# Two layers of experts: products in ordered phases of one array tiling, gathers and scatters of the last layer done another way

## The chip, the cores and the metric

One core of a Trainium2 chip runs the whole program in one launch. The metric is the device time of one execution in microseconds, the median of several runs. TensorE (PE) multiplies; a product's stationary operand is loaded by PEld beside it. DVE is VectorE, ACT ScalarE, POOL GpSimd, SP SyncE, and SPq and POOLq are the queues of DMA issues of the last two. All transfers share 16 DMA engines.

## The reference

The program is two transformer blocks on 512 tokens ("latents") of 1024 channels, with 256 tokens of context beside the first block. The first block has two layers, each a mixer (two attentions, a convolution, gates, an output product) and then a feed-forward of 16 experts, where each expert chooses its tokens; the context has the experts in layer 0 alone. The second block has two more attentions and an output product. All is float32. The change lies in the experts:

```python
def expert_choice_ffn(h, w_router, w_g, w_u, w_d):
    B, n, D = h.shape
    cap = CAPACITY_FACTOR * n // N_EXPERTS         # 64 latents, 32 of the context
    logits = jnp.einsum('bnd,de->ben', h, w_router, preferred_element_type=jnp.float32)
    aff = jax.nn.softmax(logits, axis=1)
    gate, idx = lax.top_k(aff, cap)
    bi = jnp.arange(B)[:, None, None]
    xs = h[bi, idx]
    a = jnp.einsum('becd,edf->becf', xs, w_g)      # w_g, w_u, w_d: 16 x 1024 x 1024
    u = jnp.einsum('becd,edf->becf', xs, w_u)
    y = jnp.einsum('becf,efd->becd', jax.nn.silu(a) * u, w_d)
    return jnp.zeros_like(h).at[bi, idx].add(y * gate[..., None].astype(y.dtype))
```

Here `h` is a norm of the rows with a scale and a shift per channel, and the result, times a gate per channel, is added to the rows.

## The kernel before

The kernel is written with tile pools. A scheduler in the language's compiler gives each engine its order: it takes instructions by the priority of the program's order and by when it reckons them ready, so that work of later lines can stand between work of earlier ones. Semaphores are made from the data's dependences.

**Order of the program** (`run`, from L48): mixer of layer 0 on the latents, then on the context, `experts` for both streams, mixer of layer 1 on the latents, `experts_local`, then block 2.

**Weights of the experts** (`ring_start`, `ring_open`, `ring_load`, from L834). An expert has three matrices of 4 MB: gate, up, down. They stream through a ring of slots of 2 MB, half a matrix each, ten slots in layer 0 and nine in layer 1. A load is two DMAs of 1 MB on SP's queue (L865), and waits until the products that read the slot's last content are done. The first slots are filled during the mixer that goes before.

**One expert** (`up` L1211, `act` L1222, `down_ps` L1237). The tokens' channel-major norms `xT` are stationary, the weights stream. A latent expert has 64 tokens, so two halves of the columns stand side by side in the array (tiling 128*64, `h` = 2, 512 columns each); a context expert has 32, so four quarters do (128*32, 256 columns each). Gate and up products go to PSUM, `act` makes 2 * silu(a) * u with ACT and DVE, turns it with transposes on TensorE (128*128) and copies it to SBUF, and the down product takes it as stationary.

**Layer 0** (`experts` L1269). Per expert: gate product of the latents, of the context, up product of both, `act` of both, down product of both. `gather` (L1192) fetches 128 rows (two latent experts or four of the context) by an indirect DMA on POOL's queue, transposes them in 8 pieces and applies scale and shift (`affine`). `down` (L1249) scales the output by gate and channel gate and adds it to the rows in DRAM with an indirect accumulating DMA. The latents' expert 0 goes ahead of the stage, in `expert0` (L1260).

**Layer 1** (`experts_local` L1297). The rows and their norms stay in SBUF (`kept`, filled in `project` L1016 to L1068). `gather(g)` makes a one-hot matrix of two experts' tokens and multiplies it with the four tiles of norms; `scatter(e, y)` splits the 64 x 1024 output into a high and a low part and multiplies each by a one-hot matrix, 16 products with 64 rows, whose sums DVE adds to the rows (L1350). Both halves of the output's columns lie in different halves of the partitions.

**Choice** (`choose` L1111): ranks the tokens on DVE and gives each expert's indices and gates (`ig`), and for streams that fetch by DMA the indices as integers (`gi`, `si`).

Of the kernel before, what the change touches and what calls it, by code (L numbers as in the profile page):

```python
# [8 lines left out]
FP32 = mybir.dt.float32  # L9
# [20 lines left out]
class Stream:  # L30
    """One of the two token streams: latents or context."""
# [6 lines left out]
class Kernel:  # L38
    def __init__(self, tc, A, out):
        self.tc, self.nc, self.A, self.out = tc, tc.nc, A, out  # L40
        self.uid = 0
        self.flip = 0
        self.pend = None
        self.pcols = 768
        self.late = None
        self.wada = {}

# [58 lines left out]
    def blend(*parts):  # L106
        """The steps of several (generator, steps), spread evenly over each other."""
# [22 lines left out]
    def copy(self, out, in_):  # L130
        """A plain copy, on the scalar engine and the vector engine in turn."""
# [6 lines left out]
    def transpose(self, out, in_):  # L138
        p = in_.shape[0]
        self.nc.tensor.transpose(out, in_, self.ident[:p, :p])  # L140
# [24 lines left out]
    def exp(self, pool, out, x, w):  # L165
        """exp(x) for x <= 0 on the vector engine, to float32's accuracy: 2^k * e^r, |r| <= ln(2) / 2."""
# [14 lines left out]
    def split(self, src, hi, lo):  # L181
        """src = hi + lo, both in the 12 significant bits of float32r."""
# [3 lines left out]
    def wblock(self, pool, src):  # L186
        """A block of weights [K, 256]: per 512 rows its two float32r parts [128, 4, 256]."""
# [10 lines left out]
    def mm3(self, ps, lhs, rhs, lsel, rsel):  # L198
        """ps = sum over k tiles of lhs^T rhs, each a list of two parts by k tile."""
# [70 lines left out]
    def adaln(self, l, r, pool):  # L270
        """Columns r * 2048 to (r + 1) * 2048 of both streams' modulation of layer l, in 17 steps."""
# [35 lines left out]
    def ada_load(self, l, r, pool, *tiles):  # L307
        """Loads pieces [128, 1024] of w_ada, unless they are there."""
# [18 lines left out]
    def norm(self, xt, junk, xn=None):  # L327
        """Token-major rows scaled by their rsqrt of the mean square, in place or into xn; the last tile's on its own."""
# [9 lines left out]
    def scale(self, out, in_, col, i):  # L338
        """Rows by a column, on the vector engine and the scalar engine in turn."""
# [17 lines left out]
    def hT(self, pool, h, xn, G, S):  # L357
        """The modulated norm of a stream, channel-major, in two parts; KT steps."""
# [21 lines left out]
    def hT_raw(self, raw, xn):  # L380
        """The norm without its modulation, channel-major."""
# [29 lines left out]
    def heads_block(self, pool, ps, dst, ss, t, nh, tabs, g):  # L411
        """dst = rope(ps * g) for nh heads of one token tile; ss = their sums of squares."""
# [58 lines left out]
    def k_parts(self, tp, kh, kl, j):  # L471
        """Head j of the transposed keys tp [128, n] into the doubled parts kh, kl [128, n]."""
# [6 lines left out]
    def k_block(self, pool, kr, ss, nt, nh, kh, kl):  # L479
        """Normalises the roped keys kr [128, nt, nh * 64] and writes their parts."""  # L480
# [11 lines left out]
    def kv_block(self, pool, w, h, st, tabs, g, kh, kl, V, kr=None):  # L492
        """Two key heads and two value heads of a stream from a block [ka | va] of w_in."""
# [1117 lines left out]
```

## Time and profile before

| | us |
|---|---|
| time, median of 3 runs | 3030.7 (3026.78 to 3032.99) |
| span of the profiled execution, first to last instruction | 3023.8 |
| TensorE busy | 2895.2 (96%) |
| DVE busy | 1415.6 (47%) |
| ACT busy | 957.7 (32%) |
| POOL busy | 110.1 (4%) |
| mean granted TensorE clock, as a share of full speed | 0.977 |
| bytes moved | 629.24 MB, mean 208 GB/s |

The profiled execution has no time of its own beside its span. Times in the trace are microseconds from the span's start. Matmuls are pipelined, so the busy time of one is longer than its distance to the next; where work stands in blocks, the distance between the blocks' starts is what it costs. A share of the DMA engines near 1 means that packets were in flight on all 16 throughout; it can pass 1 a little, since packets overlap.

### The profile page before, as it was taken

How to read it: one execution, taken by the hardware profiler on the slowest of the kernel's cores; microseconds unless marked ns; L12 is line 12 of the kernel's file. 1: busy time of each engine (PE TensorE's matmuls, PEld its weight loads, DVE VectorE, ACT ScalarE, POOL GpSimd, SP SyncE). 2: the span in 40 equal slices, each digit the busy share in tenths (PEclk: the TensorE clock that was granted, in tenths of full speed). 3: DMA queues.
4: the chain of work that ended last, by engine and by line, in shares of the span. 5: the costliest groups of instructions: out<-in, count | busy, mean ns of one | idle time of the engine just before them, and what ended most of it. 6: DMA issues, size and time to landing. Idle time of an engine off the chain costs nothing.

```text
span 3023.8 us, 45171 instructions
## 1 busy us (share of the span) xinstructions
PE 2895.2 (96%) x18117; PEld 1866.4 (62%) x18117; DVE 1415.6 (47%) x3807; ACT 957.7 (32%) x1950; POOL 110.1 (4%) x135
## 2 busy tenths in 40 slices
PE   7999999999998999999979999999799999889999
PEld 3777777678895443433347777778744433338878
DVE  4655565348764111111146555654523232237885
ACT  4444454224552000000044444543200000015663
POOL 0100000011001011100000000000000000000000
PEclk8999999999998999999999999999899999999999
DMA  8321111668457999999573211114689999953221
GB/s 296 123 69 56 56 42 50 206 210 308 136 174 255 389 403 397 402 395 368 180 262 116 68 56 56 43 53 141 260 348 397 414 361 363 370 196 107 57 84 57
DMA packets 272646, 629.24 MB, mean 208 GB/s; under 512 B 24324, under 2 KB 148948, under 8 KB 272436
## 3 DMA queue, kind: packets, MB, share of 16 engines
q1 hardware_dynamic: 259396, 595.31, 53.5%
q0 software_dynamic: 12016, 27.86, 3.2%
q8 instruction: 143, 2.34, 0.3%
q10 hardware_dynamic: 1024, 3.18, 0.3%
q14 instruction: 67, 0.55, 0.1%
HBM read 606.30 MB, written 19.99 MB: 207 GB/s over the span
## 4 chain that ended last, share of the span: by engine, by line
PE 73%; issue 14%; DMA 6%; DVE 4%; ACT 1%; SPq 0%; POOL 0%; POOLq 0%; ACTq 0%; DVEq 0%
PE mm L204 13%; PE mm L205 12%; PE mm L206 12%; PE au L1217 8%; PE tp L140 5%; PE yp L1243 4%; PE S L521 4%; PE mm L611 4%; DMA x<-ylat,silat 4%; PE S L520 3%; PE S L282 3%; PE tx L1330 2%; PE yp L1348 1%; DVE xt L1350 1%; PE S L1038 1%
## 5 line engine op out<-in xcount | busy, mean ns | idle before, releaser
L204 PE MATMUL mm<-hhi,whi 128*128 128x512 f32 (+1 forms) x928 | 341.6, 368 | 0.0
L184 DVE TENSOR_TENSOR wlo<-wraw,whi 128x1024 fp32r<-128x1024 f32 x234 | 285.7, 1222 | 107.0 <-ACT whi L183 102.4
L206 PE MATMUL mm<-hhi,wlo 128*128 128x512 f32 (+1 forms) x928 | 335.1, 361 | 0.0
L205 PE MATMUL mm<-hlo,whi 128*128 128x512 f32 (+1 forms) x928 | 333.6, 360 | 0.0
L183 ACT ACTIVATE whi<-wraw 128x1024 fp32r<-128x1024 f32 x234 | 247.1, 1059 | 185.5 <-PE mm L205 106.7
L1243 PE MATMUL yp<-we,hT 128*32 128x256 f32 (+1 forms) x2016 | 294.2, 496 | 10.3 <-ACT hT L134 4.9
L1217 PE MATMUL au<-we,xT 128*64 128x512 f32 x1024 | 236.5, 597 | 0.0
L204 PE MATMUL mm<-whi,hhi 128*128 128x256 f32 x736 | 218.8, 298 | 10.6 <-ACT qr L423 6.6
L1217 PE MATMUL au<-we,xTlat 128*64 128x512 f32 x960 | 227.1, 599 | 0.3
L205 PE MATMUL mm<-wlo,hhi 128*128 128x256 f32 x736 | 212.8, 290 | 2.1 <-DVE wlo L184 2.1
L206 PE MATMUL mm<-whi,hlo 128*128 128x256 f32 x736 | 212.5, 290 | 0.0
L1243 PEld LDWEIGHTS yp<-we,hT 128*32 128x32 f32 (+1 forms) x2016 | 99.1, 124 | 182.4 <-issue 144.5
L563 ACT ACTIVATE PT<-tp 128x384 f32<-128x384 f32 (+2 forms) x392 | 142.6, 407 | 211.6 <-PE tp L140 209.7
L204 PEld LDWEIGHTS mm<-hhi,whi 128*128 128x128 f32 x928 | 176.3, 190 | 32.1 <-issue 4.4
L206 PEld LDWEIGHTS mm<-hhi,wlo 128*128 128x128 f32 x928 | 176.0, 190 | 25.9 <-issue 1.1
L205 PEld LDWEIGHTS mm<-hlo,whi 128*128 128x128 f32 x928 | 176.3, 190 | 24.9 <-issue 1.5
L535 ACT ACTIVATE P<-S,mx,sc 128x768 f32<-128x768 f32 (+5 forms) x192 | 151.9, 792 | 70.9 <-DVE mx L532 67.6
L204 PEld LDWEIGHTS mm<-whi,hhi 128*128 128x128 f32 x736 | 143.0, 194 | 26.9 <-ACT qr L423 8.5
L1217 PEld LDWEIGHTS au<-we,xT 128*64 128x64 f32 x1024 | 70.6, 137 | 129.2 <-issue 126.1
L205 PEld LDWEIGHTS mm<-wlo,hhi 128*128 128x128 f32 x736 | 143.0, 195 | 5.4 <-DVE wlo L184 2.7
L206 PEld LDWEIGHTS mm<-whi,hlo 128*128 128x128 f32 x736 | 142.7, 194 | 4.0 <-issue 2.8
L1226 ACT ACTIVATE th<-au 128x512 f32<-128x512 f32 (+1 forms) x47 | 24.6, 524 | 378.3 <-PE au L1217 378.3
(326 smaller groups left out, 4830.5 us busy)
## 6 DMA issues: line engine op xcount, KB each, us to landing
we<-in_w_e_gate_dram SPq DMA_DIRECT2D x128, 1024.0 KB, 11.5
we<-in_w_e_up_dram SPq DMA_DIRECT2D x128, 1024.0 KB, 11.1
we<-in_w_e_down_dram SPq DMA_DIRECT2D x128, 1024.0 KB, 11.0
wraw<-in_w_in_dram SPq DMA_DIRECT2D x166, 512.0 KB, 3.7
wada<-in_w_ada_dram SPq DMA_DIRECT2D x96, 512.0 KB, 6.1
wraw<-in_w_branch_dram SPq DMA_DIRECT2D x36, 512.0 KB, 3.4
wraw<-in_w_out_dram SPq DMA_DIRECT2D x32, 512.0 KB, 3.9
xt<-in_x_dram SPq DMA_DIRECT2D x8, 512.0 KB, 9.2
```

Source lines behind the costliest of these rows:

```text
L140: self.nc.tensor.transpose(out, in_, self.ident[:p, :p])
L183: self.nc.scalar.activation(hi, src, ACTF.Copy)
L184: self.nc.vector.tensor_sub(lo, src, hi.bitcast(FP32))
L204: nc.tensor.matmul(ps, lh, rh, start=k == 0, stop=False)
L205: nc.tensor.matmul(ps, lh, rl, start=False, stop=False)
L206: nc.tensor.matmul(ps, ll, rh, start=False, stop=k == n)
L521: nc.tensor.matmul(S[:, at:at + w], lhs[row], kl[row, k0:k0 + w], start=False, stop=True)
L535: nc.scalar.activation(P, S[:, c0:c1], ACTF.Exp, bias=mx[:, 1:2], scale=sc, accum_out=mx[:, 2:3])
L563: self.nc.scalar.activation(PT[:, s0:s0 + j - i, qc:qc + 128], tp[:, i * 128:j * 128].rearrange("p (s c) -> p s c", c=128), ACTF.Copy)
L611: nc.tensor.matmul(O[64 * j:64 * j + 64, a:b], v, PTs[j][:, slot, a:b], start=i == 0, stop=i == last, skip_group_check=True)
L1217: self.nc.tensor.matmul(ps[j * st.cap:(j + 1) * st.cap], st.xT[:, kt, s0:s0 + st.cap], w[kt // 4][:, kt % 4, j * st.w:(j + 1) * st.w], sta ...
L1243: self.nc.tensor.matmul(ps[o * st.cap:(o + 1) * st.cap], hT[:, j * 128 + q * st.cap:j * 128 + (q + 1) * st.cap], w[kt // 4][:, kt % 4, o * ...
```

## The change

Three things. First, an order of TensorE's work in both expert stages: `pe_phase` opens a phase, and `pe_run` adds for given instructions an edge to each instruction of the phase before, without a semaphore, so that the scheduler keeps the phases apart. In layer 0 a round is: down product of the latents' last expert and gate and up products of the next (128*64); gate and up of the context and its last down product (128*32); all transposes (128*128). Fetches are issued one group ahead of the transposes that use them. In layer 1 a round is the last expert's down product and the next one's gate and up (128*64), then scatter, gather and transposes (128*128).

Second, the norms of layer 1 go to DRAM as in layer 0 (two buffers instead of four tiles kept), and `gather` is the one of layer 0. `choose` makes the integer indices for this stream too.

Third, the scatter takes two experts at once: high and low part of each half of the columns are stacked to 128 rows (`parts`), and the sums of both experts are formed in PSUM before DVE adds them, half of them after each of the next two experts. In block 2 the norm's result has tiles of its own.

The comments and docstrings that the diff takes out are left out here.

```diff
+    def pe_phase(self):
+        self.pe_before, self.pe_now = self.pe_now, []
+    def pe_run(self, insts):
+        insts = [i.ins for i in insts]
+        for i in insts:
+            for b in self.pe_before:
+                self.tc.add_manual_dep(
+                    i, b.name, mybir.DependencyInfo(mybir.DependencyClass.NoSync, mybir.DependencyReason.DATA),
+                    reason="phase")
+        self.pe_now += insts
...
 project:
-            xo = xp.tile([128, D], FP32, name="xn", bufs=nx)
+            xo = p.tile([128, D], FP32, name="xn", bufs=2)
             self.scale(xo, xt[t], r, t)
-            if dst:
-                nc.gpsimd.dma_start(self.dr[f"xn{st.name}{l}"][t * 128:t * 128 + 128], xo)
-            else:
-                self.kept.append((xt[t], xo))
+            nc.gpsimd.dma_start(self.dr[f"xn{st.name}{l}"][t * 128:t * 128 + 128], xo)
+            if not dst:
+                self.kept.append(xt[t])
...
 choose:
+        st.gi = cp.tile([128, NE // h], U32, name="gi" + sfx)
         if st.xs is not None:
+            for j in range(h):
+                nc.vector.tensor_copy(st.gi[j * cap:(j + 1) * cap],
+                                      ig[:cap, 0].rearrange("p (g j) -> p j g", j=h)[:, j])
             nc.vector.tensor_copy(ig[64:128], ig[:64])
...
-    def gather(self, st, g, p, p_x, bufs=1):
-        xg = p.tile([128, D], FP32, name="xg" + st.name, bufs=1)
-        nc.gpsimd.indirect_dma_start(
-            out=xg, out_offset=None, in_=self.dr[f"xn{st.name}{st.l}"],
+    def fetch(self, st, g, p):
+        st.xg = p.tile([128, D], FP32, name="xg" + st.name, bufs=1)
+        self.nc.gpsimd.indirect_dma_start(
+            out=st.xg, out_offset=None, in_=self.dr[f"xn{st.name}{st.l}"],
             in_offset=bass.IndirectOffsetOnAxis(ap=st.gi[:, g:g + 1], axis=0))
+    def gather(self, st, p, p_x, bufs=1):
...
 up, down_ps (the products of the first and the last k tile):
+            if kt in (0, KT - 1):
+                self.pe_run(r)
...
 act is cut in two, act (up to t) and act_turn:
+        self.pe_run([self.transpose(tp[:, j * 128:(j + 1) * 128], t[:, j * 128:(j + 1) * 128]) for j in range(nj)])
...
 experts:
+            for st in sts:
+                self.expert_setup(l, st, xs[st.name], p)
+                self.fetch(st, 0, p)
+            hT, wd = {}, None
+            def turned(st, e):
+                if e % st.h == 0 and e < NE:
+                    st.xT = self.gather(st, p, p_x, 2 if st is lat else 1)
+                    if e + st.h < NE:
+                        self.fetch(st, e // st.h + 1, p)
+            for st in sts:
+                turned(st, 0)
+            for e in range(NE + 1):
+                self.pe_phase()
+                if lat in hT:
+                    self.down(lat, wd, hT[lat], e - 1, p, p_y)
+                t = {}
+                if e < NE:
+                    w = [self.ring_get(i, e) for i in range(2)]
+                    for st in sts:
+                        if st is cx:
+                            self.pe_phase()
+                        if e or st is cx:
+                            t[st] = self.act(st, *[self.up(st, w[i], e, p_a) for i in range(2)], p)
+                if cx in hT:
+                    self.down(cx, wd, hT[cx], e - 1, p, p_y)
+                self.pe_phase()
+                if e < NE:
+                    hT = {}
+                    if lat in t:
+                        hT[lat] = self.act_turn(lat, t[lat], p, p_x)
+                    turned(lat, e + 1)
+                    hT[cx] = self.act_turn(cx, t[cx], p, p_x)
+                    turned(cx, e + 1)
+                    wd = self.ring_get(2, e)
...
 experts_local:
+            def parts(e, ps):
+                y = p.tile([128, 512], FP32, name="y")
                 nc.vector.scalar_tensor_tensor(y, in0=ps, scalar=st.ig[:, 1, e:e + 1], in1=st.gt2,
                                                op0=ALU.mult, op1=ALU.mult)
+                one = p.tile([128, NL], F32R, name="two", bufs=3)
+                nc.vector.tensor_scalar(one, row, st.ig[:, 0, e:e + 1], None, op0=ALU.is_equal)
+                yp = p.tile([128, 2, 512], F32R, name="yp", bufs=3)
+                for o in range(2):
+                    a, b = slice(64 * o, 64 * o + 64), slice(64 - 64 * o, 128 - 64 * o)
+                    nc.scalar.activation(yp[a, o], y[a], ACTF.Copy)
+                    nc.vector.tensor_sub(yp[b, o], y[a], yp[a, o].bitcast(FP32))
+                return one, yp
+            def scatter(ys, tiles):
+                for t in tiles:
+                    for o in range(2):
+                        ps = p_y()
+                        self.pe_run([nc.tensor.matmul(ps, one[:, t * 128:(t + 1) * 128], yp[:, o],
+                                                      start=i == 0, stop=i == len(ys) - 1)
+                                     for i, (one, yp) in enumerate(ys)])
+                        x = self.kept[t][:, 512 * o:512 * o + 512]
+                        nc.vector.tensor_add(x, x, ps)
+                        yield
...
+            for e in range(NE):
+                self.pe_phase()
+                if hT is not None:
+                    ys.append(parts(e - 1, self.down_ps(st, wd, hT, p_y())))
+                t = self.act(st, *[self.up(st, self.ring_get(i, e), e, p_a) for i in range(2)], p)
+                self.pe_phase()
+                if e % 2 == 0 and len(ys) == 2:
+                    work, ys = scatter(ys, range(4)), []
+                for _ in range(4):
+                    next(work, None)
+                if e % 2 and e + 1 < NE:
+                    turned(e // 2 + 1)
+                hT = self.act_turn(st, t, p, p_x)
+                wd = self.ring_get(2, e)
+            self.pe_phase()
+            ys.append(parts(NE - 1, self.down_ps(st, wd, hT, p_y())))
+            self.drive(scatter(ys, range(4)))
```

## Rows read from the trace of the kernel before

**Rows 1.** TensorE's timeline, layer 0: start us, us, line, operation, out<-in, tiling, moving operand

```profile
982.39 7.84 PE L1217 MATMUL au<-we,xTctx 128*32 128x256 f32 x128
...
1260.75 10.68 PE L1243 MATMUL yp<-we,hT 128*64 128x512 f32 x96 [0.35 <-ACT hT L134]
1271.36 7.09 PE L1217 MATMUL au<-we,xTlat 128*64 128x512 f32 x32
1278.38 3.66 PE L1217 MATMUL au<-we,xTctx 128*32 128x256 f32 x64
...
1293.98 10.68 PE L1243 MATMUL yp<-we,hT 128*64 128x512 f32 x96 [0.35 <-ACT hT L134]
1304.59 1.09 PE L140 MATMUL tx<-ident,xglat 128*128 128x128 f32 x8
```

**Rows 2.** The same timeline, the end of layer 0

```profile
1454.81 1.94 PE L1217 MATMUL au<-we,xTlat 128*64 128x512 f32 x8
1456.68 1.07 PE L1217 MATMUL au<-we,xTctx 128*32 128x256 f32 x16
...
1479.16 11.95 PE L1243 MATMUL yp<-we,hT 128*64 128x512 f32 x96 [0.35 <-ACT hT L134]
...
1515.39 11.95 PE L1243 MATMUL yp<-we,hT 128*64 128x512 f32 x96 [0.35 <-ACT hT L134]
1527.15 1.98 PE L282 MATMUL S<-wada,silu 128*32 128x512 f32 x16
```

**Rows 3.** Timeline of DVE and TensorE ahead of layer 1's experts

```profile
2151.04 0.75 DVE L343 TENSOR_SCALAR xn<-xt,rsq 128x1024 f32<-128x1024 f32 x1
...
2158.88 0.76 DVE L343 TENSOR_SCALAR xn<-xt,rsq 128x1024 f32<-128x1024 f32 x1
...
2185.79 0.17 DVE L1164 COPY ig<-ig 64x32 f32<-64x32 f32 x1
...
2197.18 14.81 PE L1217 MATMUL au<-we,xT 128*64 128x512 f32 x66
```

**Rows 4.** Timeline of TensorE and DVE in layer 1: a gather, the last expert

```profile
2302.78 10.02 PE L1330 MATMUL tx<-one,xn 128*128 128x128 f32 x64 [1.33 <-DVE one L1322]
...
2704.07 7.09 PE L1243 MATMUL yp<-we,hT 128*64 128x512 f32 x32 [0.78 <-DVE hT L136]
...
2713.99 5.29 DVE L1350 TENSOR_TENSOR xt<-xt,yp 128x512 f32<-128x512 f32 x8 [0.58 <-PE yp L1348]
```

**Rows 5.** Stretches: from:to, us, busy PE, PEld, DVE, ACT, POOL, PEclk, DMA share, GB/s

```profile
982.00:1316.00 334.00, 331.61 (x2991) 136.09 (x2993) 50.00 (x100) 29.31 (x61) 37.77 (x27) 1.00 1.03 398
...
2197.00:2330.00 133.00, 129.98 (x633) 59.90 (x633) 35.24 (x64) 11.27 (x21) 0.00 (x0) 0.96 0.95 381
2330.00:2672.00 342.00, 318.84 (x1532) 130.46 (x1530) 103.58 (x184) 23.53 (x45) 0.00 (x0) 0.98 0.97 377
...
2324.00:2412.00 88.00, 85.22 (x432) 36.67 (x430) 27.55 (x50) 6.07 (x11) 0.00 (x0) 1.00 1.03 416
...
1064.00:1072.00 8.00, 8.00 (x62) 2.88 (x61) 0.69 (x1) 0.60 (x1) 1.56 (x1) 1.00 1.06 356
```

**Rows 6.** Weight loads (L865), issue to landing: from 985 to 1085, from 1285 to 1385

```profile
DMA to landing us min/median/max: 5.8/17.9/21.1
...
DMA to landing us min/median/max: 7.3/10.9/17.8
```

**Rows 7.** Groups of layer 1's experts: line, operation, count | busy us, mean ns | idle before

```profile
L1348 PE MATMUL yp<-yhi,two 64*128 64x512 f32 x128 | 52.6, 485 | 8.7 <-DVE xt L1350 7.1 <-ACT yhi L183 1.6
L1348 PE MATMUL yp<-ylo,two 64*128 64x512 f32 x128 | 42.4, 426 | 0.9 <-DVE ylo L184 0.9
```

**Rows 8.** Indirect fetches of layer 0 (L1196), issue to landing

```profile
DMA to landing us min/median/max: 4.1/8.1/9.8
```

**Rows 9.** Stretches as in rows 5, with TensorE standing

```profile
2150.00:2180.00 30.00, 18.27 (x146) 17.47 (x143) 22.23 (x94) 5.99 (x12) 0.00 (x0) 0.75 0.68 266
...
2720.00:2750.00 30.00, 23.77 (x153) 21.41 (x154) 21.94 (x64) 16.33 (x26) 0.10 (x1) 0.81 0.47 143
```

More of the change, by code (lines that the diff above doesn't have):

```diff
@@ L1202, in gather @@
             tp = p_x()
-            for i in range(4):
-                kt = 4 * q + i
-                self.transpose(tp[:, i * 128:(i + 1) * 128], xg[:, kt * 128:(kt + 1) * 128])
+            self.pe_run([self.transpose(tp[:, i * 128:(i + 1) * 128], xg[:, (4 * q + i) * 128:(4 * q + i + 1) * 128])
+                         for i in range(4)])
             for i in range(4):
@@ L1276, in experts @@
             p_a, p_x, p_y = [lambda nm=nm: pools[nm].tile([128, 512], FP32, name=nm) for nm in ("au", "tx", "yp")]
-            for e in range(NE):
-                run = [st for st in sts if e or len(sts) == 1 or st is not self.lat]
-                for st in sts:
-                    if e == 0:
-                        self.expert_setup(l, st, xs[st.name], p)
-                    if e % st.h == 0:
-                        st.xT = self.gather(st, e // st.h, p, p_x, 2 if st is self.lat else 1)
-                a = {st.name: [] for st in run}
-                for i in range(2):
-                    w = self.ring_get(i, e)
-                    for st in run:
-                        a[st.name].append(self.up(st, w, e, p_a))
-                hT = {st.name: self.act(st, *a[st.name], p, p_x) for st in run}
-                w = self.ring_get(2, e)
-                for st in run:
-                    self.down(st, w, hT[st.name], e, p, p_y)
+            lat, cx = sts
@@ L1337, in scatter @@
-            def scatter(e, y):
-                one = p.tile([128, NL], F32R, name="two")
-                nc.vector.tensor_scalar(one, row, st.ig[:, 0, e:e + 1], None, op0=ALU.is_equal)
-                parts = [p.tile([128, 512], F32R, name=x) for x in ("yhi", "ylo")]
-                self.split(y, *parts)
-                for t in range(4):
-                    for o in range(2):
-                        a, cs = slice(64 * o, 64 * o + 64), slice(512 * o, 512 * o + 512)
-                        ps = p_y()
-                        for i, part in enumerate(parts):
-                            nc.tensor.matmul(ps, one[a, t * 128:(t + 1) * 128], part[a], start=i == 0, stop=i == 1)
-                        x = self.kept[t][0][:, cs]
-                        nc.vector.tensor_add(x, x, ps)
@@ L1352, in experts_local @@
-            st.xT = gather(0)
-            y = None
-            for e in range(NE):
-                a = []
-                for i in range(2):
-                    w = self.ring_get(i, e)
-                    a.append(self.up(st, w, e, p_a))
-                if y is not None:
-                    scatter(e - 1, y)
-                if e % 2 and e + 1 < NE:
-                    st.xT = gather(e // 2 + 1)
-                hT = self.act(st, *a, p, p_x)
-                ps = self.down_ps(st, self.ring_get(2, e), hT, p_y())
+            self.fetch(st, 0, p)
@@ L1367, in experts_local, with turned @@
                                                op0=ALU.mult, op1=ALU.mult)
-            scatter(NE - 1, y)
+                one = p.tile([128, NL], F32R, name="two", bufs=3)
[16 more added lines that the diff above has]
+                        yield
+            def turned(g):
+                st.xT = self.gather(st, p, p_x)
+                if g + 1 < NE // 2:
+                    self.fetch(st, g + 1, p)
+            turned(0)
+            hT, ys, work = None, [], iter(())
+            for e in range(NE):
[15 more added lines that the diff above has]
+            self.drive(scatter(ys, range(4)))
         for q in reversed(self.rpools):
@@ L1388, in block2 @@
             with self.sb("in2", side="right") as p:
-                xt, xn = zip(*self.kept)
+                xt = self.kept
+                xn = [p.tile([128, D], FP32, name="xn", bufs=nt) for _ in range(nt)]
                 for t in range(nt):
```

62 lines of the change are left out of this document (19 added, 43 removed).

## The prediction

> **What bounds the kernel now.** I read TensorE's timeline through both expert stages first. The experts of layer 0 run from 982.4 us, where the stage's first product starts [rows 1], to 1527.15, where the next stage's follows [rows 2]: 544.8 us. Those of layer 1 run from 2197.2 [rows 3] to the last add's end at 2719.3 [rows 4]: 522 us. Then the stretches: in both stages TensorE is busy nearly throughout, and so are the DMA engines, with a share of 1.03 and 398 GB/s in layer 0, 0.95 to 0.97 and about 380 GB/s in layer 1, and 416 GB/s there where the share is 1.03 without a break [rows 5]. The reader is to see two bounds that lie close together: what one engine gains, the other may take back.
>
> Which of the two is it? In layer 0 an expert whose tokens need no gather takes 1260.75 to 1293.98 = 33.2 us, and TensorE stands only 0.35 us in it, for a copy [rows 1]. The weights' landing times shrink from a median of 17.9 us to 10.9 [rows 6]: the queue before the DMA engines gets shorter, so the stream is a little faster than TensorE, about 7 us in 300, or 33 us per expert. TensorE is the bound, by a few per cent. Late in the stage the two streams' products come in alternation, and the same expert takes 1479.16 to 1515.39 = 36.2 us [rows 2].
>
> In layer 1 a pair of experts pays 64 products for its gather (2302.78, 10.02 us, [rows 4]) and 32 for its scatter (52.6 + 42.4 us in the stage, 5.9 us per expert, [rows 7]). TensorE sets the pace: 522/16 = 32.6 us per expert, and the DMA share is below 1 because no slot is free.
>
> **The change, part by part.**
>
> *Layer 0, phases.* Alone, 32 products of the latents take 1271.36 to 1278.38 = 7.02 us, and the 96 of a down product of both streams 1260.75 to 1271.36 = 10.61, so 64 of the context take 3.59 [rows 1]. An expert has three blocks of each: 31.83 us. Fifteen of these and the first expert's context (10.77) are 488.2. Transposes: 15 x 6 + 2 for the hidden rows, 7 x 8 + 3 x 8 for the gathers, 172 at 1.09/8 us [rows 1]: 23.4. Changes of tiling: between two others, 8 latent products take 1454.81 to 1456.68 = 1.87 us [rows 2] against 8 x 7.02/32 = 1.755, so 0.115 each; three per expert, 48 in all: 5.5. (The late experts have some 17 each now.) Waits: the latents' down product opens the next phase and needs the copy of its hidden rows. That costs 0.35 us now [rows 1]; then the copy has only the context's two transposes (0.27) as cover in experts without a gather. Ends: 0.35 and 1.4 per expert; I take 0.65, nearer to the row, 10.4 in all. Sum: 488.2 + 23.4 + 5.5 + 10.4 = 527.5, against 544.8: **-17 us** (-22 to -5).
>
> A point against it: a slot is now free only when the context has used it, in the second phase, and all six of an expert come free within some 11 us. With ten slots, the up weights of expert e + 1 wait for the down slots of e - 1, the last to be freed. They land after some 3 us of latency and two slots of 5 us, 13 us, and are wanted after transposes, down and gate product, 2 + 7 + 7 = 16. That holds by 3 us. The stream itself needs 33 us per expert against TensorE's 34. If it lags, each expert follows the stream, and the gain here goes to nothing: that is a case below.
>
> The fetches go out a group earlier. On POOL's queue the scatters of the same expert stand behind them, but their outputs come some 7 us of matmul later; a fetch that waits for its buffer waits on transposes just passed. Nothing, then; without that cover the issue itself, 1 us x 10. At the end the latents' down product runs 3.6 us ahead of the context's, so their scatter and the next layer's first load leave earlier: **-2** (-3.6 to 0).
>
> *Layer 1, before the stage.* The normalised rows now go through two buffers to DRAM, so the third tile's scaling on DVE (2158.88) waits for the write of the first (scaled at 2151.04, [rows 3]). A landing of 4.1 to 9.8 us, the nearest row [rows 8], would hold DVE by 0 to 3 us, and the row sums and the router's adds queued behind it with it; TensorE waits for those. The tokens' column falls away on SP. The first gather: indices are ready at 2185.96, two small casts (0.17 each) are added, then issue to landing 4.1 to 9.8 (median 8.1, [rows 8]), then 8 transposes, 1.1, and as much again for the affine (estimate): 2192.6 to 2198.3, 2196.6 at the median; now it is 2197.2 [rows 3]. Together **0** (-4 to +4).
>
> *Layer 1, gathers and scatters.* The 64 products, their one-hot compares and index broadcasts go; 8 transposes remain (1.1). Scatter: 16 products per pair instead of 32, each 128 rows deep. The trace has none of this shape in the stage; at the same time each as now they are 3 us per expert, at twice that 5.9; I take 3, since the columns streamed by each are the same. The adds on DVE halve. TensorE per expert: 21.06 for up and down, 3, 0.5 for transposes of hidden rows, 0.55 for the gather, 0.3 for changes of tiling, 0.8 for the copy: 26 us (29 at the other end).
>
> So something else is late next: the weights. An expert has 12.58 MB, at 416 GB/s [rows 5] 30.2 us, and its share of a gather (0.26 MB) 0.6. With 26 against 30.8 TensorE eats up the nine slots' lead within some ten experts and then waits. The stage's end is the stream's: the first half matrix is used at 2197.2 + 3.5 = 2200.7; 87 slots of 2.097 MB, 5.04 us each, 438.5; seven gathers of 0.524 MB, 8.8; first landing 3 us (landings are 5.8 at least for 1 MB [rows 6], less 2.5 to move it). That is 2651. Then the last half of a down product, 3.5, and from its end to the last add 8.1 as now (2711.16 to 2719.28, [rows 4]), plus 0.6 for one more split on ACT: 2663.2, **-56 us**. At 398 GB/s, as beside the scatters of layer 0, it would be -36; TensorE at 29 us changes nothing.
>
> Sum: -17 - 2 + 0 - 56 = -75, from a span of 3023.8 to 2949. The profiled execution has no time of its own beside its span; the median of the runs is 6.9 us above it, their lowest 3.0, their highest 9.2. With the median's distance: **2956 us**.
>
> **Rivals.**
>
> *Layer 0 gains nothing* (0.20). The slots are freed in one burst, or the phases leave TensorE waiting at their boundaries, or the added edges do not keep the two streams apart, so that the change doesn't do what it says. For it: the stream there needs 33 us of 34. Against: landings had 7 us to spare at the end. 3030.7 - 56 = 2974.
>
> *The clock falls* (0.05), the slower side. Waiting for weights some 5 us per expert in layer 1, TensorE is no longer busy throughout. The granted clock is 0.75 where it is busy 18.3 of 30 us and 0.81 at 23.8 of 30 [rows 9]; the new stage has about 26 of 31. [...]
> [...] Here the two stretches with the lower shares are those where TensorE stands for longer than I expect in the new stage.
>
> *The stream is slower than that* (0.02). With 356 GB/s, as beside two scatters of layer 0 [rows 5], a slot takes 5.89 us: 2200.7 + 87 x 5.89 + 10.3 + 3 + 12.2 = 2739, +19, and with the -19 of layer 0 and the handover nothing is left: 3031. Against: 416 GB/s over 88 us.
> [...]
>
> *Layer 1 stays TensorE's* (0.04): the stream is faster with a deeper queue. 16 x 26 + 9 = 425, -97, in all -116: 2915. Against: layer 0 had the deeper queue and no more than 398.
>
> **How the numbers follow.** My case has 0.69: 2956, on its own 2942 (-22, -3.6, -4, and -59 without the first landing's latency) to 2985 (-5, 0, +4, and -45, half-way to the 398 GB/s end). The range for 8 in 10 takes in the second case and the 398 GB/s end: 2934 to 2992. The measurement can't tell less than 0.2% (6 us) from no change. Faster: 0.69 + 0.20 + 0.04 = 0.93; same 0.02; slower 0.05.
>
> **What would show it.** Layer 0: a 7.0 us block of down and two of up for the latents in one piece, then the context's, then transposes, 34 us per expert to the end; the stage some 527 us. Layer 1: DMA share above 1 from the first freed slot to the end, no gap in it; TensorE waiting for the weights, some 5 us per expert, from about the tenth expert; landings of the weights growing above 20 us; 64 adds on DVE instead of 128; the stage near 466 us. Wrong: a layer 1 whose DMA share stays below 1 (TensorE still the bound), a granted clock below 0.8 there, landings in layer 0 that grow, TensorE waiting there for the up weights, or a first gather that lands after 2198.

## The result and the profile after

The changed kernel takes 2958.9 us (median of 4 runs, 2957.96 to 2961.82), the kernel before beside it 3031.8 (4 runs, 3026.78 to 3033.85): a ratio of 0.9767, 95% interval 0.9753 to 0.9781, 72.9 us less. The forecast was 2956, with 2934 to 2992.

Both programs take 1.8 us more than their span (2961.82 against 2960.0 in the profiled execution of the changed kernel), so the profile of before belongs to an execution of about 3025.6 us, faster than its median, and the profile of after belongs to its slowest run, 2.9 us above its median. Between the two profiles 63.8 us are gone. They divide as follows; the times of before stand in [rows 1 to 4], but for its mixer's first row transposes, at 1550.15.

| stretch | before | after | difference | forecast |
|---|---|---|---|---|
| up to the first context product of layer 0's stage | 982.4 | 981.9 | -0.5 | 0 |
| layer 0's stage, to the next product behind it | 544.8 | 525.2 | -19.6 | -17 |
| from there to the mixer's first row transposes | 23.0 | 23.3 | +0.3 | -2 |
| from there to layer 1's first gate product | 647.0 | 651.6 | +4.6 | 0 |
| layer 1's stage, to the last add's end | 522.1 | 475.1 | -47.0 | -56 |
| the rest, block 2 | 304.5 | 303.0 | -1.5 | 0 |

Each column is one execution. A second profile of the changed kernel (`e11_changed_again`, below) has 985.6, 522.9, 23.5, 648.7, 475.3 and 302.9 us in the same stretches, so a difference of 2 to 4 us in one stretch can be that of two executions. Layer 1's 47 us and layer 0's 20 stand far above it; the mixer's 4.6 do not.

**Layer 0.** TensorE's timeline after (columns as in [rows 1]): its beginning, one round and the end.

```profile
981.85 9.02 PE L1234 MATMUL au<-we,xTctx 128*32 128x256 f32 x128
...
1294.70 7.09 PE L1264 MATMUL yp<-we,hT 128*64 128x512 f32 x32
1301.62 13.90 PE L1234 MATMUL au<-we,xTlat 128*64 128x512 f32 x64
1315.45 7.11 PE L1234 MATMUL au<-we,xTctx 128*32 128x256 f32 x128
1322.38 3.64 PE L1264 MATMUL yp<-we,hT 128*32 128x256 f32 x64
1325.95 0.88 PE L141 MATMUL tx<-ident,th 128*128 128x128 f32 x6
1327.35 7.09 PE L1264 MATMUL yp<-we,hT 128*64 128x512 f32 x32 [0.53 <-ACT hT L135]
...
1496.59 10.68 PE L1264 MATMUL yp<-we,hT 128*64 128x512 f32 x96 [0.53 <-ACT hT L135]
1507.09 1.03 PE L297 MATMUL S<-wada,silu 128*32 128x512 f32 x4
```

Each line is one whole block: three of the latents, three of the context, six transposes, and again. The round from 1294.70 takes 32.65 us, a late one like an early one. The last line but one is a block of 96: at the end both streams' down products are one phase.

**Layer 1.** The same timeline: the first gather and its products, three rounds' starts (their down products), the first wait for weights, the last expert.

```profile
2180.11 1.97 PE L141 MATMUL tx<-ident,xglat 128*128 128x128 f32 x8 [6.12 <-DMA xglat<-xnlat,gilat]
2182.01 14.84 PE L1234 MATMUL au<-we,xTlat 128*64 128x512 f32 x64
...
2198.99 7.18 PE L1264 MATMUL yp<-we,hT 128*64 128x512 f32 x32
...
2223.85 7.08 PE L1264 MATMUL yp<-we,hT 128*64 128x512 f32 x32
...
2247.90 7.09 PE L1264 MATMUL yp<-we,hT 128*64 128x512 f32 x32 [0.75 <-ACT hT L135]
...
2320.95 1.94 PE L1234 MATMUL au<-we,xTlat 128*64 128x512 f32 x8 [0.62 <-DMA we<-in_w_e_up_dram]
...
2616.69 1.94 PE L1234 MATMUL au<-we,xTlat 128*64 128x512 f32 x8 [0.50 <-DMA we<-in_w_e_gate_dram]
2619.26 1.94 PE L1234 MATMUL au<-we,xTlat 128*64 128x512 f32 x8 [0.63 <-DMA we<-in_w_e_gate_dram]
2621.82 1.94 PE L1234 MATMUL au<-we,xTlat 128*64 128x512 f32 x8 [0.62 <-DMA we<-in_w_e_gate_dram]
```

The first rounds take 24.9 and 24.1 us. From 2320.95 on the gate and up products, wherever TensorE has caught up with the loads, come in groups of eight, one every 2.56 us: eight products read one load of 1.049 MB, and 1.049 MB in 2.56 us is 410 GB/s. TensorE does 1.94 us of work on each and waits 0.6 for the next. The windows of the stage (columns as in [rows 5]) say the same from the other side, and so does the weights' time from issue to landing, from 2282 to 2382:

```profile
2212.00:2312.00 100.00, 93.83 (x432) 35.97 (x430) 26.46 (x44) 11.86 (x22) 1.87 (x2) 0.98 1.03 409
2312.00:2412.00 100.00, 83.61 (x372) 28.64 (x368) 24.36 (x42) 9.98 (x19) 1.87 (x2) 0.98 1.03 409
...
2512.00:2612.00 100.00, 82.73 (x368) 29.72 (x368) 26.65 (x46) 9.98 (x19) 0.94 (x1) 0.98 1.03 409
```
The landings:

```profile
DMA to landing us min/median/max: 18.1/18.4/19.9
```

The DMA share is 1.03 (1.02 in the window left out) where it was 0.95 to 0.97 [rows 5], the rate is 409 GB/s in every window, and the 18.4 us from issue to landing are some seven loads of 2.56 us each. TensorE's busy time falls to 83%; its granted clock stays at 0.97 to 0.98.

### The profile page after: what moved, and what is told of

Its sections match the earlier page's. It is cut to its first block, busy times and chain, and to the rows that moved or that the text cites. A ratio compares the mean times of both kernels' runs of the same rounds, so it can differ in the third digit from the quotient of the medians.

```text
span 2960.0 us, 43855 instructions
## 1 busy us (share of the span) xinstructions
PE 2782.5 (94%) x17509; PEld 1841.2 (62%) x17509; DVE 1376.1 (46%) x3729; ACT 966.7 (33%) x1966; POOL 119.8 (4%) x147
## 5 line engine op out<-in xcount | busy, mean ns | idle before, releaser
L1234 PE MATMUL au<-we,xTlat 128*64 128x512 f32 x1984 | 451.0, 596 | 36.2 <-DMA we<-in_w_e_up_dram 23.5
L1234 PEld LDWEIGHTS au<-we,xTlat 128*64 128x64 f32 x1984 | 156.6, 137 | 320.0 <-issue 207.1
L1264 PE MATMUL yp<-we,hT 128*32 128x256 f32 (+1 forms) x2016 | 287.7, 494 | 14.5 <-ACT hT L135 7.3
L1264 PEld LDWEIGHTS yp<-we,hT 128*32 128x32 f32 (+1 forms) x2016 | 112.3, 125 | 167.6 <-issue 110.8
L221 PEld LDWEIGHTS mm<-hhi,wlo 128*128 128x128 f32 x928 | 176.2, 190 | 26.1 <-issue 1.1
L1246 DVE SCALAR_TENSOR_TENSOR th<-th,au 128x512 f32<-128x512 f32 (+1 forms) x47 | 28.1, 597 | 248.4 <-ACT th L1245 248.4
```

Of the source, the lines that this page charges most:

```text
L221: nc.tensor.matmul(ps, ll, rh, start=False, stop=k == n)
L1234: r = [self.nc.tensor.matmul(ps[j * st.cap:(j + 1) * st.cap], st.xT[:, kt, s0:s0 + st.cap], w[kt // 4][:, kt % 4, j * st.w:(j + 1) * st.w] ...
L1264: r = [self.nc.tensor.matmul(ps[o * st.cap:(o + 1) * st.cap], hT[:, j * 128 + q * st.cap:j * 128 + (q + 1) * st.cap], w[kt // 4][:, kt % 4 ...
```

## Experiments

Each ran beside the kernel before on one chip, which lay at 3020 to 3039 us there with medians of 3028.8 to 3032.4. Stage times are those of the profiled execution, cut as in the table above. The edits are shown in short.

**Layer 0 alone, layer 1 alone.** The change is divided: in the first kernel `project`, `choose` and `experts_local` are those of before, in the second `experts` is.

```diff
 e1_layer0_phases: experts_local
-    (the changed kernel's)
+    (before's: one-hot gather, scatter expert by expert)
 e2_layer1_only: experts
-    for e in range(NE + 1): self.pe_phase() ...
+    for e in range(NE): gather, up of both, act of both, down of both
```

> Only layer 0 has the ordered phases and the earlier fetches; layer 1 is gathered and scattered with one-hot matrices as before. Theory (the two layers' gains add up; layer 0's is TensorE's saved changes of tiling and waits): layer 0's stage near 525 us as in the changed kernel, layer 1's near 522 as before, 18 to 21 us below the kernel before in all, a ratio of 0.993 to 0.994. Rival (some of what layer 0 gains is given back in the mixer or at layer 1's start): stage near 525 but less than 12 us in all.

> Only layer 1 is changed (phases there, fetches by indirect DMA, scatters in pairs); layer 0 has the order of before. Theory (layer 1's stage follows the weights' stream at 409 GB/s, whatever was gained ahead of it): its stage near 475 us, 45 to 53 us below the kernel before in all, a ratio near 0.984. Rival (layer 1's stage was shorter since layer 0 left the queues or the clock in a better state): less than 40 us gained, a stage above 485.

Layer 0 alone: 3009.5 us, ratio 0.9925 (0.9897 to 0.9953), 21.1 us less; its stage 522.7, layer 1's 521.6. Layer 1 alone: 2983.0, ratio 0.9846 (0.982 to 0.9872), 47.6 less; stages 544.5 and 476.0. The sum of the two is 68.8, with the whole at 72.9: the gains stand in separate places and add up within what the runs scatter, and both rivals fall. Layer 0 alone also shows something else: its mixer takes 651.1 us, as long as the changed kernel's, though its layer 1 is that of before.

**No phases.**

```diff
     def pe_run(self, insts):
+        if not self.ordered:        # False throughout
+            return
```

> The changed kernel without the phases' edges in both layers; the program's order, the earlier fetches, the gathers by DMA and the paired scatters stay. Theory: layer 0 loses its gain, 12 to 20 us, because changes of tiling come back; layer 1 loses less than 5 us, since it waits for the weights and has 5 us per expert to spare; in all 53 to 62 us below the kernel before, where the changed kernel has 73. Rival A (layer 0's gain is the earlier fetch, not the phases): within 5 us of the changed kernel. Rival B (without phases layer 1 becomes TensorE's again): over 30 us above the changed kernel, with layer 1's stage above 490.

2983.5 us, ratio 0.9844 (0.9816 to 0.9872), 47.1 us less than the kernel before, some 24 us above the changed kernel. Its layer 0 takes 544.1, as before; its layer 1 473.8, no longer than with the edges. Some 6.5 us more are lost ahead of layer 0's stage, which starts at 988.5, and the whole lies outside the 53 to 62 expected; the changed kernel's second profile starts it at 985.6, so that half of these can be scatter between executions. The late rounds of layer 0 in this kernel, TensorE's timeline:

```profile
1462.45 1.94 PE L1236 MATMUL au<-we,xTlat 128*64 128x512 f32 x8
1464.32 1.50 PE L1266 MATMUL yp<-we,hT 128*32 128x256 f32 x22
1465.75 5.37 PE L1236 MATMUL au<-we,xTlat 128*64 128x512 f32 x24
1471.05 1.48 PE L1236 MATMUL au<-we,xTctx 128*32 128x256 f32 x18
1472.46 1.94 PE L1236 MATMUL au<-we,xTlat 128*64 128x512 f32 x8
```

The alternation of [rows 2] is back, though the fetches still go out early. So layer 0's gain is the edges' alone, and in layer 1 they are worth nothing that shows. Whether it is the changes of tiling or something else in the alternation that costs, the edges do not separate.

**Half of the stream.** From layer 1's third expert on the kernel leaves half of the weights out.

```diff
-        for j in range(2):
+        for j in range(1 if self.rl == 1 and e >= 2 else 2):
             self.nc.sync.dma_start(t[:, 2 * j:2 * j + 2], src[:, 2 * j:2 * j + 2])
 up, down_ps:
-    w[kt // 4][:, kt % 4, ...]
+    w[kt // 4][:, kt % m, ...]      # m = 2 for these experts
```

> From the third expert of layer 1 on each slot gets half of its bytes (its first 1 MB), and the products of its other k tiles read the loaded half again; the number of products, slots and waits is the same. Theory (the stage follows the stream): TensorE sets the pace with the 26 us per expert that it has ahead of its first wait for weights; the stage 16 x 26 + 9 = 425 us, some 45 to 55 us below the changed kernel, 118 to 128 below the kernel before; no wait for weights. Rival (the stage is bound by the chain of slots, copies and products, 29 us per expert and more on TensorE): the stage stays above 460.

2903.4 us, ratio 0.9587 (0.9556 to 0.9618), 127.2 below the kernel before; layer 1's stage 417.8. Two windows of it:

```profile
2312.00:2412.00 100.00, 95.36 (x437) 37.82 (x435) 28.27 (x49) 11.25 (x22) 1.87 (x2) 1.00 0.74 252
2412.00:2512.00 100.00, 95.37 (x428) 40.12 (x426) 28.84 (x49) 11.16 (x21) 1.87 (x2) 0.98 0.73 252
```
What TensorE waited for in the stage (who waited for whom: us in total, times, longest):

```profile
PE tx L141 <- ACT xTlat L1120: 15.3, 7, 2.3
PE yp L1265 <- DVE hT L137: 1.3, 1, 1.3
PE yp L1379 <- DVE yp L1371: 0.9, 1, 0.9
```

No wait for weights is left, the DMA share falls to 0.74, and TensorE needs 417.8/16 = 26.1 us per expert with all its waits for scale, shift and copies. The stage of 475.1 us is the weights'; 57 us of it are TensorE's reserve, 3.6 per expert.

**Scatter as before, and more products.** The first takes back the paired scatter; the second adds as many products as the one-hot gather had.

```diff
 e5_single_scatter: scatter
-    matmul(ps, one[:, t], yp[:, o]) for both experts, 128 rows, one add
+    matmul(ps, one[a, t], part[a]) for (yhi, ylo), 64 rows, an add per expert
 e6_more_products: turned
+    ps = p_x()
+    for k in range(8):
+        self.pe_run([self.transpose(ps[:, i % 4 * 128:i % 4 * 128 + 128], st.xg[:, i * 128:i * 128 + 128])
+                     for i in range(8)])
     st.xT = self.gather(st, p, p_x)
```

> The changed kernel with the scatter of the kernel before (32 products of 64 rows and 16 adds per expert's pair of halves, each expert by itself); the gather stays an indirect DMA. Theory (the weights' stream is the bound): TensorE needs 26.1 us per expert, as with half of the stream, and 2.9 more, 29.0 in all, just under the stream's 29.7; layer 1's stage 475 to 480 us, the whole within 6 us of the changed kernel's 2959. Rival (each product that is left out shortens the stage): 16 x 2.9 = 47 us longer, a stage of 520.

> The changed kernel, and in layer 1 ahead of each gather's transposes 64 more 128x128 transposes on TensorE that nobody reads, as many products as the one-hot gather of before had, without its other work. 64 x 0.137 = 8.8 us for two experts. Theory (TensorE at 26.1 us per expert has 3.6 us to spare against the stream's 29.7): 26.1 + 4.4 = 30.5 us, so TensorE is the bound again by a little; stage 9 + 16 x 30.5 = 497 us, 15 to 25 us above the changed kernel. Rival (the reserve is larger, the waits for weights hide it all): a stage under 480. Rival (no reserve): 16 x 4.4 = 70 us, a stage of 545.

The single scatter: 2964.7 us, ratio 0.9781 (0.9764 to 0.9798), stage 479.2, with 128 adds on DVE. The products that the pairing saves are worth some 4 us here and not 47. TensorE is busy for 91 to 97% in its windows at the same 409 GB/s, and its waits in the stage are:

```profile
PE tx L141 <- ACT xTlat L1120: 18.4, 7, 2.6
PE yp L1264 <- DVE hT L137: 4.7, 6, 0.8
PE au L1234 <- DMA we<-in_w_e_up_dram: 3.6, 7, 0.6
```

Waits for weights of 3.6 us are left of 37.3: the two bounds meet here. The other half, the one-hot gather with the paired scatter, was not tried.

More products: 2972.5 us, ratio 0.9804 (0.9787 to 0.9822). I had expected a stage of 497; it is 474.9. Two groups of them, with the next wait (TensorE's timeline):

```profile
2181.93 10.64 PE L141 MATMUL tx<-ident,xglat 128*128 128x128 f32 x72 [6.25 <-DMA xglat<-xnlat,gilat]
...
2229.48 8.08 PE L141 MATMUL tx<-ident,xglat 128*128 128x128 f32 x72
2239.11 0.66 PE L141 MATMUL tx<-ident,th 128*128 128x128 f32 x4 [1.56 <-ACT xTlat L1120]
```

72 transposes in a row take 8.08 us, 7.0 more than eight do, and the wait behind them is 0.8 us shorter than in the changed kernel: 3.1 us per expert and not 4.4, 29.2 with the 26.1, still under the stream's 29.7. My price, the mean of a short group, was too high. The profiled execution is 13.9 us longer than the changed kernel's. Half of that, 6.9 us, lies where there is no cover: ahead of the stage's first product, where the 72 transposes take 10.64 us instead of the 1.97 of eight. The rest, 3.1 us ahead of layer 0's stage and 3.4 in block 2, is far from the edit.

**The wait in the second mixer.** Between layer 0's end and layer 1's first product the changed kernel is 4.6 us slower, though its first gather is some 4 us quicker there. SP's queue in the kernel before:

```profile
2090.53 14.15 SPq L191 DMA_DIRECT2D wraw<-in_w_out_dram  x3
2104.86 0.37 SPq L1024 DMA_DIRECT2D gt<-mod  x1
```
In the changed kernel:

```profile
2074.17 20.12 SPq L206 DMA_DIRECT2D wraw<-in_w_out_dram  x5
2094.34 0.50 SPq L1039 DMA_DIRECT2D gt<-mod  x1
```

And DVE's timeline there:

```profile
2099.83 0.76 DVE L1094 TENSOR_TENSOR py<-mm,gt 128x256 f32<-128x256 f32 x2 [4.25 <-DMA gt<-mod]
```

The scheduler now puts the projection's gate (`gt`) behind five blocks of weights on SP, not three; DVE waits 4.25 us for it and TensorE 3.1 for DVE. Every kernel with the new layer 1 that leaves this load alone has the wait, 3.8 to 4.8 us; the kernel before and the one with layer 0's change alone have not. The wait is not the whole of the 4.6 us: layer 0 alone has none of it and takes 651.1 us all the same. TensorE stands in that stretch for as long as before (21.2 us, 21.1 before); what it loses there is clock, some 4 us by the estimate of the last section (13 against 9).

```diff
 e7_gate_on_act (both layers), e9_turns_gate_router (the second line too):
-        nc.sync.dma_start(gt, ...)
+        nc.scalar.dma_start(gt, ...)
-        nc.sync.dma_start(wr, ...)
+        nc.scalar.dma_start(wr, ...)
```

> The changed kernel with one DMA issued on another queue: the mixer's output gate (gt, 4 KB to all rows) goes out on ACT's queue, not on SP's behind five blocks of weights. Theory (the 3 us that TensorE waits in the second mixer for DVE, and DVE for this gate, come from the gate's place on SP's queue): no wait for gt; from the first row transposes after the experts of layer 0 to the first product of layer 1's experts 3 us less than the 648 to 652 us of the kernels with the layer-1 change; the whole 2 to 4 us below the changed kernel. Rival (the weights of w_out are as late as the gate): the same wait falls to them, no change.

2964.4 us, ratio 0.9784 (0.9769 to 0.9799): no gain. The wait for `gt` is gone; the router's weights, next on the same queue, are as late. The two longest of the waits for it, by DVE and by TensorE:

```profile
DVE gw L1060 <- DMA wr<-in_w_router_dram: 5.6, 1, 5.6
...
PE S L1052 <- DMA wr<-in_w_router_dram: 4.1, 1, 4.1
```

**Hidden rows turned first.** In layer 0 the context's transposes wait for a PSUM tile that the gathered rows hold.

```diff
                     if lat in t:
                         hT[lat] = self.act_turn(lat, t[lat], p, p_x)
-                    turned(lat, e + 1)
                     hT[cx] = self.act_turn(cx, t[cx], p, p_x)
+                    turned(lat, e + 1)
                     turned(cx, e + 1)
```

> The changed kernel, and in layer 0 both streams' hidden rows are transposed ahead of the gathers' transposes. They wait now for a PSUM tile that ACT's scale and shift of the gathered rows holds (9.6 us in the stage). Theory (TensorE is the bound in layer 0): stage 6 to 10 us shorter, 515 to 519, the whole 6 to 10 us below the changed kernel. Rival (the weights' stream is as late there): stage within 2 us of 525.

> The changed kernel with three moves: in layer 0 both streams' hidden rows are transposed ahead of the gathers' transposes, and both mixers' output gate (gt) and router weights (wr) are issued on ACT's queue, not on SP's behind the blocks of weights. Theory (the 3 us of TensorE's wait for gt fell to wr, which stood next on SP's queue, when gt alone was moved; with both moved nothing is left of it): no wait for gt or wr; 3 to 4 us less than with the changed kernel between layer 0's end and layer 1's first product, and 7 us less in layer 0's stage: 2947 to 2951 us. Rival (TensorE's clock takes it back: each stretch in which it goes to half speed costs 1.5 us and more, wherever it falls): the waits go, the time stays above 2954.

> The changed kernel itself, beside the two others on the same chip, to see how far its own runs lie apart. All theories: 2955 to 2965 us, layer 1's stage 475, layer 0's 522 to 526.

Turns first: layer 0's stage 518.3 us, 4.6 to 6.9 less than in the changed kernel's two profiles. TensorE's largest wait in the stage, in the changed kernel:

```profile
PE tx L141 <- ACT xTlat L1120: 9.6, 8, 1.3
```
And in this one:

```profile
PE tx L141 <- ACT xTlat L1120: 4.5, 3, 1.5
```

All its waits for other engines in layer 0's stage fall from 14.4 to 11.3 us, since those for ACT's copies of the hidden rows grow by 2. So layer 0 is still TensorE's: what it gains there, the stage gains. The whole, 2958.5 us (2951.68 to 2963.22, ratio 0.9756, 0.9737 to 0.9775), can't be told from the changed kernel, which ran again at 2959.5 (2957.48 to 2968.42, ratio 0.9772, 0.9751 to 0.9792). In the profiled execution block 2 took 3 us more than in the changed kernel's, at a lower granted clock (0.85 against 0.89 in its first 40 us).

Turns, gate and router: 2962.5 us, ratio 0.9776 (0.9759 to 0.9793), which neither theory had. From layer 0's end to layer 1's first product it is 641.2 us, 10 less than the changed kernel, but only 3 of these are waits (TensorE stands for 25.9 us there, not 28.8); the other 7 are, by the estimate of the last section (5 us against 13), falls of its clock that did not come. Layer 0's stage takes 519.5; but that stage starts at 1001.5 instead of 981.9. I had moved the loads in layer 0's mixers as well, and there it did harm. TensorE's two largest waits from 500 to 985, where the changed kernel has 2.3 us for `wr` and none for `py`:

```profile
PE S L1052 <- DMA wr<-in_w_router_dram: 8.7, 1, 8.7
PE mm L219 <- DVE py L1094: 4.6, 1, 4.6
```

They are 11 us more than in the changed kernel, of the 19.6. Most of the rest is clock: by the estimate of the last section it costs 28 us ahead of the stage, and 19 in the changed kernel.

**Longer pieces.** Is 409 GB/s what these loads can reach? Each partition gets two neighbouring rows of a matrix, 8 KB in a piece.

```diff
-        src = src.rearrange("(k p) f -> p k f", p=128)
+        src = src.rearrange("(q p k) f -> p q k f", p=128, k=2)
         for j in range(2):
-            self.nc.sync.dma_start(t[:, 2 * j:2 * j + 2], src[:, 2 * j:2 * j + 2])
+            self.nc.sync.dma_start(t[:, 2 * j:2 * j + 2], src[:, j])
```

> The changed kernel, and each partition of an expert's weight slot gets two neighbouring rows of the matrix, so that the contiguous pieces of a load are 8 KB long and not 4 KB; as many bytes, loads and slots. The rows of a product's k tiles are then not those of its stationary operand: the experts compute something else. Theory (the stream's 409 GB/s is a rate of bytes): layer 1's stage within 5 us of 475. Rival (a part of it is a price per piece, and so the stage's bound is the form of the loads): a higher rate, the stage 5 to 30 us shorter, at most down to TensorE's 418.

2952.5 us, ratio 0.974 (0.9721 to 0.9759), layer 1's stage 462.9, 12 less. A window of it:

```profile
2312.00:2412.00 100.00, 88.42 (x388) 31.16 (x384) 26.30 (x45) 11.24 (x21) 1.88 (x2) 0.95 1.01 421
```

The rate goes from 409 to 421 GB/s, and 475.1 x 409/421 = 461.6. The rival has it: the form of the loads is a part of the bound.

**All together.** Turns first; gate and router weights on ACT's queue in layer 1 alone; and the longer pieces with the stationary operands in the same order of rows, so that the reference is computed again.

```diff
+        eng = nc.scalar if l else nc.sync       # for gt and wr
 gather, act_turn: transposes of every second column
-    self.transpose(tp[...], xg[:, (4 * q + i) * 128:(4 * q + i + 1) * 128])
+    self.transpose(tp[...], x.rearrange("t (a p b) -> t a b p", a=n // 2, b=2)[:, i // 2, i % 2])
+    scale and shift of the experts in that order, by four products per stream (affine_pairs)
```

> The changed kernel with what the runs point to: hidden rows transposed ahead of the gathers in layer 0; gate and router weights of layer 1's mixer alone on ACT's queue; and expert weights in 8 KB pieces, now with the stationary operands in the same order of rows, so that the reference is computed (the transposes take every second column, and scale and shift are put into that order by four small products per stream). Theory (the three gains lie in different stretches and add up): layer 0's stage 518 to 520 us, 641 to 644 us from there to layer 1's first product, layer 1's stage 462 to 465; 2930 to 2938 us in all. Rival (with layer 0's TensorE faster its stream is late, or the small products and strided transposes cost what the pieces gain): layer 0's stage above 522 or layer 1's above 468, 2942 us or more.

2943.3 us (2941.47 to 2951.66), ratio 0.9731 (0.9712 to 0.9749): the best version, 16 us below the changed kernel, though above the 2930 to 2938 expected. This is the rival's time, though not its stages: the parts lie near what they were to give, layer 0's stage 521.0, then 24.1 and 642.8, layer 1's stage 464.0. TensorE waits 1.8 and 3.0 us for the inputs of the new small products, and block 2 took 306.2 us instead of 303, again at a lower clock (by the estimate of the last section it costs 5 to 6 us there instead of 2 to 3).

## Why the prediction came out, step by step

- **Layer 0, -17, measured -19.6.** The mechanism is shown: the stage is 544 without the edges and 525 with them, and the fetches ahead give nothing. The waits at the boundaries, put at 10.4 us, are 14.4 (9.6 + 2.1 + 2.1 + 0.6), most of them in another place than I had it: not the latents' copy, but the PSUM tile that the gathered rows hold. The stage is shorter than the sum's 527.5 all the same, because the other terms were off as well. The blocks of products take some 484 us in all, not 493.7 with their changes of tiling: a round's are 31.25 (1294.70 to 1325.95), and I had 31.83 and 0.35. The transposes and waits between them take some 41, not 33.8. The case that the stream takes the gain back did not occur; the weights' landings grew, to a median of 16 to 20 us after the first 100. I had named that as a sign of being wrong, and it was none: TensorE waited for none of the loads.
- **Handover, -2, measured +0.3.** Wrong, by a misreading of the code: in the last round no phase stands between the two streams' down products, and they ran as one block of 96. The latents' outputs did not leave earlier.
- **Before layer 1's stage, 0, measured +4.6.** Three things lie in it. The first gather landed 4.2 us after its issue, not at the median of 8.1, and the way from the indices to the first product is some 4 us shorter (6.9 from the last copy of `ig`, 11.2 before). DVE waits nowhere for the writes of the norms (0 of the 0 to 3). But SP's queue was reordered around the projection, which I had passed over with "the tokens' column falls away on SP": 3.1 us on TensorE. Of the other 6 or so 4 are TensorE's clock, by the estimate below (13 us against 9); layer 0 alone, with 12, shows that such falls need no change of layer 1.
- **Layer 1, -56, measured -47.0.** The mechanism holds: the stream sets the end, TensorE has 26 us of work per expert (26.1 measured), the adds halve to 64, the share is 1.02 to 1.03. The term that was mis-sized is the slot's time: 2.097 MB at 409 GB/s are 5.13 us, not 5.04, and 87 of them 446.1, not 438.5, 7.6 of the 9 us. I had taken 416 from one stretch of 88 us. The first slot was freed 4.6 us into the stage, not 3.5. TensorE first waited in the sixth expert, not the tenth, and the landings stayed at a median of 18 to 19 us, not above 20.
- **The clock** stayed at 0.97 to 0.98 in the stage's windows, with waits of 0.7 us at most for weights, but for one of 1.1. That rival had the waits, 37.3 us for weights in all, and not their form: the stream's pauses came in pieces, one behind each load. What longer ones would do to the clock there was not shown.
- **The stream at 356 GB/s** did not come: it runs at 409 in every window of the stage, and at 421 with longer pieces.
- **The sum.** -75 against the -63.8 between the two profiles: too much by 9 in layer 1, 5 in the mixer and 2 at the handover, too little by 4 to 5 in layer 0, at the start and in block 2. That the forecast came within 3 us all the same is luck: to its span it added 6.9 us for the way to the median, and the changed kernel's median lies 1.1 us below the span of its profiled execution, which makes up for 8 of the 11. The 6.9 were 1.8 of fixed distance and 5 of scatter. The medians differ by 72.9: the profile of before was of an execution some 6 us faster than its median, that of after of one 3 us slower.

## What to carry over

Where two bounds lie close together, work out the pace of both alone; what the second leaves is the gain, and what is saved beyond it is reserve. Here taking back the paired scatter cost some 4 us of 47, and as many products as the one-hot gather had cost the stage nothing: most of either saving is reserve. A change to a scheduled program moves other things too: compare the order of every queue, also far from the edit, before a step is put at nothing. A second profile of the same kernel tells which differences of a few us are worth a cause. And read a rate from the longest unbroken stretch there is.

## What the runs showed of the hardware

**The clock's short falls.** In stretches of a few us TensorE's granted clock goes from 1.00 of full speed to 0.50, while its work is the same. The second mixer in the changed kernel, two windows that follow each other; in the second the clock is 0.50 in every half microsecond from 1631.0 to 1634.0, and 1.00 from 1634.5 on:

```profile
1620.70:1630.70 10.00, 9.89 (x42) 6.95 (x42) 6.02 (x7) 4.75 (x7) 0.00 (x0) 1.00 0.34 105
1630.70:1636.00 5.30, 5.30 (x18) 4.14 (x18) 2.41 (x7) 2.16 (x4) 0.00 (x0) 0.68 0.00 0
```
The window of before that answers to the second:

```profile
1650.00:1654.00 4.00, 4.00 (x21) 3.29 (x21) 2.71 (x7) 2.16 (x4) 0.00 (x0) 1.00 0.00 0
```

A product of 128x512 follows the last every 0.43 us at 0.50 instead of 0.23, and 1.6 us are lost. TensorE had been busy for 9.89 of the 10 us before. Other falls stand at 1867 (0.56 in 7.7 us, where before has 0.72 in 6.0) and 2147 (0.67 in 8 us). The kernels of the estimate below all lose some time to them, and in partly other places (at 1650 the kernel before has 1.00); with 5 to 13 us in one stretch they are a part of what makes a 5 us gain hard to see in the medians (the changed kernel's own runs lie up to 11 us apart). What sets them off was not tried.

What they cost can be estimated: TensorE's busy time in slices of 10 us, each times what its granted clock lacks of full speed. From the second mixer's first row transposes to layer 1's first product that is 9 us in the kernel before, 12 with layer 0's change alone, 13 in the changed kernel and 9 in its second profile. It is 5 in the two kernels that issue gate and router weights on ACT's queue there, so that most of their gain in this stretch is clock; whether the move or chance did it is open. In block 2 of the kernels with the new layer 1 it is 2 to 3 us where that takes 303 us, and 5 to 6 where it takes 306.

**Pieces of 4 and of 8 KB.** 409 and 421 GB/s, at DMA shares of 1.03 and 1.01: of these two streams the faster has the lower share.
